# A decoder layer's output projection as seven products of quarters, with the gating branch's values and mixing moved behind the first stage

## The chip, the cores and the metric

The kernel runs on one core of a Trainium2 chip. A core has a tensor engine for matmuls (TensorE, PE in the profile; its loading of stationary operands is PEld), three engines for elementwise work, VectorE (DVE), ScalarE (ACT) and GpSimd (POOL), and a queue engine, SyncE (SP), from which nearly all loads are issued here. Each engine works through its own list of instructions in order; between engines, semaphores say when an operand is ready or a buffer free. The metric is the device time of one execution in microseconds. Less is better.

## The reference

One layer over 512 tokens of width 2048. All arithmetic is in float32.

```python
shift, scale, gate = split(silu(c) @ w_ada + b_ada, 3)
h = rms_norm(x, norm_g) * (1 + scale) + shift
u, v, g_a, q, k, v_b, g_b, f = split(h @ w_in)    # 7 parts of 1024 columns, 16 of f
# A: 8 channel groups of 128; v normalized over its 1024 channels, then mixed over
#    the 128 tokens of a chunk by a lower-triangular matrix per group
y_a = gelu(u) * (mix(layer_norm(gelu(v)), tril(w_s)) + b_s) * silu(g_a)
# B: 16 heads of 64, causal attention, logits biased by the running sum of log sigmoid(f + b_f)
y_b = forgetting_attention(q, k, v_b, f) * silu(g_b)
y = concat([y_a, y_b]) @ w_out                    # (512, 2048) @ (2048, 2048)
out = rms_norm(x + gate * y, final_g)
```

## The kernel before

Every float32 matrix product is done as three matmuls in a rounded format: each operand is split into a rounded part (hi) and the remainder (lo), and hi·hi, lo·hi and hi·lo are added up in PSUM. So each weight tile goes through three steps in `w_tile` (L117): a load from HBM to a `raw` buffer (a ring of 4), a copy to hi on ScalarE (L129), a subtraction for lo on VectorE (L130), or on GpSimd in the first stage. hi and lo have two buffers each. A weight tile of 128x1024 is 512 KB. The activations are split the same way (`split`, L65 to L67) and kept: `hh`/`hl` for the normalized input, `yh`/`yl` for the concatenated branches, 16 blocks of 128 channels x 512 tokens each.

Products come in two layouts. `col_group` (`mm_cols`, L145 to L147) puts 128 output columns on the partitions and the 512 tokens on the free axis; `mm_toks` (L154 to L156) puts 128 tokens on the partitions and up to 512 columns on the free axis. Either way a matmul is 128x128 by 128x512.

The program runs in these stages:

1. Normalization and transposition of x, and the sums for shift and scale.
2. The first stage (names `s`, 28 to 191 us): u and most of gate A, 14 blocks of columns, paced by loads. u becomes `y[0..7]`, gated in place.
3. `v_group(0)`, `qk_group(0)`, `g_group(0)`, then for u = 1, 2, 3 `g_group(u)`, `qk_group(u)`, `v_group(u)`: the B branch, four heads per u. After each `qk_group` the attention's steps go into a list `slots`; one entry is popped per weight tile (`tick`, L133), so attention runs among the products. Another list, `fillers`, is popped in the same way and holds `spatial_weights` (L607: loads, masks, transposes and splits the mixing matrices) at u = 1 and then the sums for the output gate (L593, L594, on GpSimd, 276 to 523 us). Attention's result is multiplied by gate B (`sgB`) and becomes `y[8..15]`.
4. The values of branch A (`va`, 610 to 706 us): 16 weight tiles, GELU, layer norm; the square root's reciprocal is a power on GpSimd (L91).
5. The last two blocks of gate A (`ga`, 706 to 730 us), with the normalization (`norm_half`), the mixing (`mix_head`, L731 to L743) and the splits of y (`split_y`) among them and at the start of stage 6.
6. The output projection (`wo`): for column groups g = 0, 1, 2 of 512 columns, eight weight tiles of two channel blocks by `mm_toks` into four banks (128 tokens each). `wo_evac` (L775) multiplies by the gate (L785), adds x (L791), squares and sums on ScalarE (L793) and multiplies by `final_g` (L795), all elementwise work in SBUF on VectorE.
7. Column group 3 is done token block by token block (L833 to L835) from weights `w3` that were loaded and split ahead, so that only the last block's scaling follows the last matmul: sum of squares, a power on GpSimd (L841), scaling (L842 to L847), output.

A scheduler sets the order on every engine. It walks the program with estimated times and priorities; weight tiles have a raised one (`WPRI`) and evacuations of PSUM too (`EPRI`), so they may be put ahead of work that was written earlier. The order lists below show what came out.

## Time and profile before

| | us |
|---|---|
| median of 3 runs | 920.67 (920.17 to 920.79) |
| the profiled execution | 922.11 |
| its span | 920.4 |
| TensorE busy in it | 898.9 |
| VectorE, ScalarE, GpSimd busy | 528.7, 412.4, 326.4 |
| mean granted TensorE clock | 0.988 of full |

The profile is of one execution, whose own time stands in the table beside the span from its first to its last recorded instruction. "L154 PE MATMUL wo<-whi_wo,yh" is line 154's matmul into the tile `wo`; after the shapes come the count, the busy sum and the mean of one in nanoseconds, then the idle time ahead and what ended it. In a timeline the first two numbers are the start and the length in microseconds; a bracket gives the idle time ahead and its releaser. In a window row the length comes first, then for PE, PEld, DVE, ACT and POOL the busy time and the count, then the clock, the share of the DMA engines and GB/s. A row of waits gives the sum, the count and the longest.

### The profile page before, as it was taken

The page shows a single profiled execution, that of the slowest core. Times are in us where ns is not written, and L with a number is a line of the kernel's source. Part 1 is how long each engine was busy: PE and PEld are TensorE (multiplying, and loading weights), DVE is VectorE, ACT ScalarE, POOL GpSimd, SP SyncE. Part 2 cuts the span into 40 slices and gives each one's busy share as a digit, 9 for nine tenths or more (in the row PEclk, how much of TensorE's full clock was granted, in tenths as well). Part 3 has the DMA queues.
Part 4 walks back from the last instruction along what each step waited for, and adds up shares of the span by engine and source line. Part 5 has one row for each costly group of instructions (what it writes and reads, how often), then busy time and mean ns, then how long its engine had stood idle before and what let it go on. Part 6 is the DMA issues. An engine that isn't in the chain of part 4 may idle for free.

```text
span 920.4 us, 12414 instructions
## 1 busy us (share of the span) xinstructions
PE 898.9 (98%) x4504; PEld 763.0 (83%) x4504; DVE 528.7 (57%) x886; ACT 412.4 (45%) x724; POOL 326.4 (35%) x238
## 2 busy tenths in 40 slices
...
PEclk8899999999999999999999999999999999999999
...
GB/s 341 352 353 355 354 302 189 76 89 136 94 114 115 130 170 145 154 150 127 160 172 179 144 81 107 78 70 92 71 107 97 81 125 105 149 180 196 69 104 92
DMA packets 113821, 142.74 MB, mean 155 GB/s; under 512 B 8400, under 2 KB 85408, under 8 KB 113248
## 3 DMA queue, kind: packets, MB, share of 16 engines
...
HBM read 137.54 MB, written 4.19 MB: 154 GB/s over the span
## 4 chain that ended last, share of the span: by engine, by line
PE 95%; DMA 2%; issue 1%; DVE 1%; ACT 0%; SPq 0%; POOLq 0%; POOL 0%; ACTq 0%; DVEq 0%
PE s L145 6%; PE s L147 6%; PE s L146 6%; PE wo L156 5%; PE wo L154 5%; PE wo L155 5%; PE vb L155 3%; PE vb L156 3%; PE vb L154 3%; PE k L145 3%; PE k L147 3%; PE gb L145 3%; PE gb L146 3%; PE k L146 3%; PE va L156 3%; PE gb L147 3%
## 5 line engine op out<-in xcount | busy, mean ns | idle before, releaser
L593 POOL TENSOR_SCALAR gate<-gate,sc 128x512 f32<-128x512 f32 x60 | 104.4, 1750 | 37.4 <-DMA gate<-in_w_ada_dram 34.5
L130 POOL TENSOR_TENSOR wlo_st<-raw_st,whi_st 128x1024 fp32r<-128x1024 f32 (+3 forms) x36 | 68.5, 1904 | 59.6 <-ACT whi_st L129 55.7
L145 PE MATMUL s<-hh,whi_st 128*128 128x512 f32 x224 | 88.0, 396 | 1.4 <-ACT hh L267 1.4
L146 PE MATMUL s<-hl,whi_st 128*128 128x512 f32 x224 | 88.1, 393 | 0.0
L594 POOL TENSOR_TENSOR gate<-gate,gate 128x512 f32<-128x512 f32 x60 | 86.5, 1442 | 2.1
L244 DVE SCALAR_TENSOR_TENSOR acc<-ada,sc,acc 128x512 f32<-128x512 f32 x98 | 73.9, 755 | 5.8 <-DMA ada<-in_w_ada_dram 3.1
L147 PE MATMUL s<-hh,wlo_st 128*128 128x512 f32 x224 | 76.4, 395 | 0.0
L154 PE MATMUL wo<-whi_wo,yh 128*128 128x512 f32 x192 | 74.8, 390 | 0.0
L155 PE MATMUL wo<-whi_wo,yl 128*128 128x512 f32 x192 | 74.7, 389 | 0.0
L155 PE MATMUL vb<-whi_vb,hl 128*128 128x256 f32 (+1 forms) x256 | 72.1, 287 | 0.0
L154 PE MATMUL vb<-whi_vb,hh 128*128 128x256 f32 (+1 forms) x256 | 71.8, 286 | 0.0
L156 PE MATMUL wo<-wlo_wo,yh 128*128 128x512 f32 x192 | 70.0, 390 | 0.0
L156 PE MATMUL vb<-wlo_vb,hh 128*128 128x256 f32 (+1 forms) x256 | 67.7, 285 | 0.0
L91 POOL TENSOR_TENSOR rsv<-rsv,nhalf 128x1 f32<-128x1 f32 x4 | 4.6, 1150 | 166.1 <-DVE rsv L90 166.1
L129 ACT ACTIVATE whi_st<-raw_st 128x1024 fp32r<-128x1024 f32 (+3 forms) x36 | 31.2, 870 | 66.3 <-PE s L146 40.9
L841 POOL TENSOR_TENSOR sfin<-sfin,nhalf 128x1 f32<-128x1 f32 x4 | 2.2, 549 | 149.0 <-DVE sfin L838 149.0
L145 PE MATMUL k<-hh,whi_k 128*128 128x512 f32 x128 | 51.1, 399 | 1.8 <-DVE q L445 1.8
L145 PEld LDWEIGHTS s<-hh,whi_st 128*128 128x128 f32 x224 | 42.6, 191 | 10.1 <-ACT hh L267 1.5
L146 PE MATMUL q<-hl,whi_q 128*128 128x512 f32 x128 | 50.7, 396 | 0.0
L145 PE MATMUL q<-hh,whi_q 128*128 128x512 f32 x128 | 50.4, 394 | 0.0
L146 PE MATMUL gb<-hl,whi_gb 128*128 128x512 f32 x128 | 50.3, 393 | 0.0
L145 PE MATMUL gb<-hh,whi_gb 128*128 128x512 f32 x128 | 50.3, 393 | 0.0
...
## 6 DMA issues: line engine op xcount, KB each, us to landing
ada<-in_w_ada_dram SPq DMA_DIRECT2D x128, 256.0 KB
...
```

Of the source, the lines that this page charges most:

```text
L91: nc.gpsimd.tensor_tensor(dst, dst, nhalf[:, 0:1], ALU.pow)
L129: nc.scalar.activation(hi, raw, AF.Copy)
L130: (loeng or nc.vector).tensor_tensor(lo, raw, hi.bitcast(F32), ALU.subtract)
L145: nc.tensor.matmul(pt, hi[:, j, cs], hh[k], start=(k == first), stop=False)
L146: nc.tensor.matmul(pt, hi[:, j, cs], hl[k], start=False, stop=False)
L147: nc.tensor.matmul(pt, lo[:, j, cs], hh[k], start=False, stop=(k == last))
L154: nc.tensor.matmul(o, ah[k][:, tsl], hi[:, j, :], start=(k == first), stop=False)
L155: nc.tensor.matmul(o, al[k][:, tsl], hi[:, j, :], start=False, stop=False)
L156: nc.tensor.matmul(o, ah[k][:, tsl], lo[:, j, :], start=False, stop=(k == last))
L244: nc.vector.scalar_tensor_tensor(sb if kk == KB - 1 else a, ga[:, j], col, a, ALU.mult, ALU.add)
L593: nc.gpsimd.tensor_scalar(ga[:, j], ga[:, j], sc[:, kk : kk + 1], None, ALU.mult)
L594: nc.gpsimd.tensor_tensor(a, a, ga[:, j], ALU.add)
```

## The change

The output projection is written as a product of 2x2 blocks and computed with seven block products instead of eight, by a known scheme. Rows of y are halved into tokens 0 to 255 and 256 to 511, channels into branch B's 1024 ("1") and branch A's ("2"), and for each pair of column groups (g1, g2) = (0, 1), (2, 3), called a unit, the weights into B11, B12 (branch B's rows), B21, B22 (branch A's). The left-hand blocks needed are A11, A12, A22 and four sums, S1 to S4; the right-hand ones B11, B21, B22 and four sums. The names p1 to p7 are those of the products: A11·p1, A12·p2, S4·p3, A22·p4, S1·p5, S2·p6, S3·p7. Each product is 256 tokens x 1024 channels x 512 columns in two banks (V, Z or X).

- **Left-hand sums.** `split_b` turns the second token half of `y[8+i]` into a difference on GpSimd before it is split; `sums` makes S1, S2, S4 from y in place on VectorE and splits them into buffers of q and k, which are free by then.
- **Right-hand sums.** p7 needs B12 and B22, loaded to `raw`, and B12 - B22 in a tile T (L912, VectorE), which is split; then T becomes B11 - T, is split again for p6 without a load, serves p5 (B22 loaded again, minus T), and becomes B21 - T for p4. Subtractions for p5 and p4 are half on VectorE, half on GpSimd. lo of p1, p2, p3, p6 is half on GpSimd as well. There are 24 loads of 512 KB per unit, 48 in all, where there were 32.
- **Alternation.** The first two products go step by step, a step of A11·p1 and one of S3·p7, since p7's T takes p1's B11 too; A12·p2 and A22·p4 likewise with B21.
- **Evacuation.** V and Z of the first two products are copied by ScalarE (c1, c7); sums u2, u3 and c7 are made on VectorE and GpSimd; gating, adding x (now on GpSimd) and squares follow per block of tokens. In unit 1 S4·p3 comes last, token block by token block, from `w3` split ahead.
- **Order of the stages.** The values (`va_products`) with `spatial_weights` come right after the first stage, and normalization and mixing lie in the slots of `v_group(0)`. The constant rows of q and k (`heads_tiles`, memsets on GpSimd) follow that. `g_group(3)` comes last before the projection, after `ga`; attention of u = 3 then ends before its gate is there, and `evac_gb` multiplies `y[14]`, `y[15]` later.

TensorE, start of the projection. Before (`wo0_t` is the bank of 128 tokens t, `whi_wo0_8` the first weight tile, `yh8` branch B's first block):

```order
L154 MATMUL wo0_0_6725<-whi_wo0_8_6731,yh8_6691 128x512
L155 MATMUL wo0_0_6725<-whi_wo0_8_6731,yl8_6692 128x512
L156 MATMUL wo0_0_6725<-wlo_wo0_8_6732,yh8_6691 128x512
L154 MATMUL wo0_0_6725<-whi_wo0_8_6731,yh9_6695 128x512
L155 MATMUL wo0_0_6725<-whi_wo0_8_6731,yl9_6696 128x512
L156 MATMUL wo0_0_6725<-wlo_wo0_8_6732,yh9_6695 128x512
```

The same place now, the second step of unit 0 (`woV` is A11·p1, `woZ` S3·p7):

```order
L849 MATMUL woV0_0_6811<-whi_p1_0_1_6884,yh10_6664 128x512
L850 MATMUL woV0_0_6811<-whi_p1_0_1_6884,yl10_6665 128x512
L849 MATMUL woV0_1_6812<-whi_p1_0_1_6884,yh10_6664 128x512
L850 MATMUL woV0_1_6812<-whi_p1_0_1_6884,yl10_6665 128x512
L849 MATMUL woZ0_0_6813<-whi_p7_0_1_6918,yh10_6664 128x512
L850 MATMUL woZ0_0_6813<-whi_p7_0_1_6918,yl10_6665 128x512
L849 MATMUL woZ0_1_6814<-whi_p7_0_1_6918,yh10_6664 128x512
L850 MATMUL woZ0_1_6814<-whi_p7_0_1_6918,yl10_6665 128x512
L851 MATMUL woV0_0_6811<-wlo_p1_0_1_6885,yh10_6664 128x512
L851 MATMUL woV0_1_6812<-wlo_p1_0_1_6885,yh10_6664 128x512
```

A step has 24 matmuls from two weight tiles of two blocks, as many as one weight tile had before; half of them wait for p7.

VectorE in the same steps, now (`ta0` is T, `p1_0_0` a raw tile of B11, `b12_0_1` and `b22_0_1` the raw tiles of the second step, `sgA`/`sgB` the gates):

```order
L67 TENSOR_TENSOR wlo_p7_0_0_6855<-ta0_6845,whi_p7_0_0_6854 128x512 x2
L355 SCALAR_TENSOR_TENSOR y6_1740<-sgA6_6611,y6_1740 128x512
L346 SCALAR_TENSOR_TENSOR sgA7_6616<-th_a7_6617,ga_1_6338 128x512
L346 SCALAR_TENSOR_TENSOR sgB6_6797<-th_b6_6798,gb3_0_6621 128x512
L912 TENSOR_TENSOR ta0_6845<-p1_0_0_6815,ta0_6845 128x512 x2
L355 SCALAR_TENSOR_TENSOR y7_1811<-sgA7_6616,y7_1811 128x512
L912 TENSOR_TENSOR ta0_6845<-b12_0_1_6912,b22_0_1_6914 128x512 x2
L441 TENSOR_TENSOR y14_6378<-y14_6378,sgB6_6797 128x512
L346 SCALAR_TENSOR_TENSOR sgB7_6802<-th_b7_6803,gb3_1_6622 128x512
L67 TENSOR_TENSOR wlo_p1_0_1_6885<-p1_0_1_6882,whi_p1_0_1_6884 128x512
L67 TENSOR_TENSOR wlo_p7_0_1_6919<-ta0_6845,whi_p7_0_1_6918 128x512 x2
```

Before, one L130 subtraction stood there per weight tile; now six operations per step make p7's operand and T, among the gatings of the last blocks of both branches.

VectorE at the end, before (`r3_3` is the last column group of the last 128 tokens):

```order
L785 TENSOR_TENSOR r3_3_7964<-wo3_3_7710,gate_141 128x512
L791 TENSOR_TENSOR r3_3_7964<-r3_3_7964,xr3_3_7966 128x512
L838 SCALAR_TENSOR_TENSOR sfin_6724<-ssf_6723,sfin_6724 128x1
L842 SCALAR_TENSOR_TENSOR r3_3_7964<-r3_3_7964,sfin_6724,fg3_7761 128x512
L845 TENSOR_SCALAR r0_3_7073<-r0_3_7073,sfin_6724 128x512
```

And now (`tmp0` and `tmp1` are the evacuations of the last product for token blocks 0 and 1, `c70`, `u30` blocks 2 and 3):

```order
L864 TENSOR_TENSOR tmp0_8236<-woZ1_0_7578,gate_141 128x512
L1020 TENSOR_SCALAR sfin_6808<-sfin_6808 128x1
L891 TENSOR_SCALAR c70_0_7084<-c70_0_7084,sfin_6808 128x512
L891 TENSOR_SCALAR u30_0_7184<-u30_0_7184,sfin_6808 128x512
L1035 TENSOR_TENSOR wide_7849<-tmp0_8236,wide_7849 128x512
L891 TENSOR_SCALAR c70_1_7085<-c70_1_7085,sfin_6808 128x512
L891 TENSOR_SCALAR u30_1_7185<-u30_1_7185,sfin_6808 128x512
L1037 SCALAR_TENSOR_TENSOR sfin_6808<-ssf_6807,sfin_6808 128x1
L889 SCALAR_TENSOR_TENSOR wide_7849<-wide_7849,sfin_6808,fgb_7282 128x512
L891 TENSOR_SCALAR c10_0_7080<-c10_0_7080,sfin_6808 128x512
L864 TENSOR_TENSOR tmp1_8280<-woZ1_1_7579,gate_141 128x512
```

The last evacuation now has the scaling of the other three token blocks ahead of it.

The diff, cut to its core:

```diff
...
+            if b > 5:
+                nc.vector.tensor_tensor(y[8 + b], y[8 + b], sg, ALU.mult)
...
+    fillers.append(spatial_weights)
+    va_products()
+    slots.extend([
+        [c_(norm_half, 0)],
+        [c_(mix_head, 0), c_(mix_head, 1)],
+        [c_(mix_head, 2), c_(mix_head, 3)],
+        [c_(norm_half, 1)],
+        [c_(mix_head, 4), c_(mix_head, 5)],
+        [c_(mix_head, 6), c_(mix_head, 7)],
+    ])
+    v_group(0)
+    heads_tiles()
+    qk_group(0)
+    g_group(0)
+    for u in range(1, 4):
...
+        if u < 3:
+            g_group(u)
+        qk_group(u)
+        v_group(u)
...
+    def split_b(i):
+        b = y[8 + i]
+        nc.gpsimd.tensor_tensor(b[:, hi_half], b[:, hi_half], b[:, lo_half], ALU.subtract)
+        split_y(8 + i)
 
     def split_y(k):
         yh[k] = act.tile([P, S], F32R, tag="hh", name=f"yh{k}")
         yl[k] = act.tile([P, S], F32R, tag="hl", name=f"yl{k}")
-        split(yh[k], yl[k], y[k], nc.gpsimd if k in (1, 3, 5, 7) else None)
-
-    norm_half(0)
-    c_ = lambda f, *a: (lambda: f(*a))
+        split(yh[k], yl[k], y[k], nc.gpsimd if k % 2 else None)
+    def sums(i):
+        b, a = y[8 + i], y[i]
+        nc.vector.tensor_tensor(b[:, hi_half], b[:, hi_half], a[:, hi_half], ALU.add)
+        nc.vector.tensor_tensor(b[:, lo_half], b[:, lo_half], b[:, hi_half], ALU.add)
+        sh_[i] = pb.tile([P, S], F32R, name=f"sh{i}", tag="qstk", bufs=8)
+        sl_[i] = pb.tile([P, S], F32R, name=f"sl{i}", tag="kstk", bufs=8)
+        split(sh_[i], sl_[i], b, nc.gpsimd if i % 2 else None)
+        nc.vector.tensor_tensor(b[:, lo_half], a[:, lo_half], b[:, hi_half], ALU.subtract)
+        s4[i] = act.tile([P, 2, H], F32R, name=f"s4_{i}", tag="ya", bufs=8)
+        split(s4[i][:, 0], s4[i][:, 1], b[:, lo_half])
...
+        [c_(split_b, i) for i in range(4)], [c_(split_b, 4), c_(split_b, 5)],
+        [c_(split_y, i) for i in range(4)], [c_(split_y, 4), c_(split_y, 5)],
     ])
-    col_group([(G0 + 768, 256)], [(lambda pt, b=b: evac_g(b, pt, pb)) for b in range(6, 8)], "ga")
-
-
-    KO = list(range(8, 16)) + list(range(8))
-    for k in KO[:8]:
-        split_y(k)
+    g_group(3)
+    slots.extend([
+        [c_(split_b, 6), c_(split_b, 7)], [c_(split_y, 6), c_(split_y, 7)],
+    ] + [[c_(sums, i)] for i in range(8)])
...
+    def wsplit(src, name, eng=None):
+        hi = wp.tile([P, 2, 512], F32R, tag="whi", name=f"whi_{name}")
+        lo = wp.tile([P, 2, 512], F32R, tag="wlo", name=f"wlo_{name}")
+        for j in range(2):
+            split(hi[:, j, :], lo[:, j, :], src[:, j, :], eng if j else None)
+        return hi, lo
...
+    def product(banks, kind, weights, begin, steps=range(4)):
+        for i2 in steps:
+            with tc.high_priority(offset=WPRI):
+                hi, lo = weights(i2)
+            for j in range(2):
+                for tt in range(2):
+                    i = 2 * i2 + j
+                    mm_part(banks[tt], kind, i, tt, hi[:, j, :], lo[:, j, :], begin and i == 0, i == 7)
             tick()
...
+        def minus(dst, a, b, pool=True):
+            for j in range(2):
+                (nc.gpsimd if j and pool else nc.vector).tensor_tensor(
+                    dst[:, j, :], a[:, j, :], b[:, j, :], ALU.subtract
+                )
+            return dst
...
+        def w_p1(i):
+            b11[i] = raw(1, g1, "p1", i)
+            return wsplit(b11[i], f"p1_{u}_{i}", nc.gpsimd)
+
+        def w_p7(i):
+            if i == 0:
+                t4 = pb.tile([P, 4, 512], F32, name=f"ta{u}", tag="vs")
+                T.extend([t4[:, 0:2, :], t4[:, 2:4, :]])
+                T.append(pb.tile([P, 2, 512], F32, name=f"tb{u}", tag="pth"))
+                T.append(pb.tile([P, 2, 512], F32, name=f"tc{u}", tag="ptl"))
+            minus(T[i], raw(1, g2, "b12", i), raw(0, g2, "b22", i), False)
+            w = wsplit(T[i], f"p7_{u}_{i}")
+            minus(T[i], b11[i], T[i], False)
+            return w
+
+        def w_p6(i):
+            return wsplit(T[i], f"p6_{u}_{i}", nc.gpsimd)
+
+        def w_p5(i):
+            a = raw(0, g2, "p5", i)
+            return wsplit(minus(a, a, T[i]), f"p5_{u}_{i}")
...
+        def w_p4(i):
+            return wsplit(minus(T[i], b21[i], T[i]), f"p4_{u}_{i}")
...
+        Z = [bank("mm" if u else "x", f"woZ{u}_{t}") for t in range(2)]
+        for i in range(4):
+            product(V, "A11", w_p1, i == 0, [i])
+            product(Z, "S3", w_p7, i == 0, [i])
+        c1 = tiles("c1", "yb", 8) if u else tiles("c1", "th")
+        evac(lambda t: nc.scalar.activation(c1[t], V[t], AF.Copy))
+        c7 = tiles("c7", "yb", 8) if u else tiles("c7", "p")
+        evac(lambda t: nc.scalar.activation(c7[t], Z[t], AF.Copy))
+        X = [bank("x", f"woX{u}_{t}") for t in range(2)]
+        product(X, "S2", w_p6, True)
...
+        evac(lambda t: nc.vector.tensor_tensor(u2[t], X[t], c1[t], ALU.add))
+        both(lambda t: nc.gpsimd.tensor_tensor(u3[t], u2[t], c7[t], ALU.add))
+        both(lambda t: nc.gpsimd.tensor_tensor(c7[t], c7[t], c1[t], ALU.add))
+        product(Z, "S1", w_p5, True)
+        evac(lambda t: nc.vector.tensor_tensor(u3[t], Z[t], u3[t], ALU.add))
...
+        for i in range(4):
+            product(V, "A12", w_p2, False, [i])
+            product(X, "A22", w_p4, False, [i])
+        evac(lambda t: gated(c1[t], V[t], g1))
+        evac(lambda t: nc.vector.tensor_tensor(c7[t], X[t], c7[t], ALU.add))
+        both(lambda t: gated(c7[t], c7[t], g1))
+        both(lambda t: piece(c1[t], t, g1))
+        both(lambda t: piece(c7[t], 2 + t, g1))
...
+        for t in range(2):
+            tk = 2 + t
+            s0, s1 = sfin[:, tk, 0:1], sfin[:, tk, 1:2]
+            nc.vector.reduce_sum(s0, ssf[:, tk, 0:4], AX.X)
+            nc.vector.tensor_scalar(s1, s0, 1.0 / D, EPS, ALU.mult, ALU.add)
+            scale_out(tk, None)
...
+            tmp = pb.tile([P, S], F32, name=f"tmp{t}", tag="sgB", bufs=3)
+            gated(tmp, Z[t], g2)
+            nc.vector.tensor_tensor(u2[t], tmp, u2[t], ALU.add)
+            squares(u2[t], t, g2, tmp)
+            nc.vector.scalar_tensor_tensor(s1, ssf[:, t, g2 : g2 + 1], 1.0 / D, s0, ALU.mult, ALU.add)
+            scale_out(t, g2)
...
```

299 lines of the change are left out of this document (174 added, 125 removed).

## The prediction

> **What bounds the kernel now.** I read the busy shares first, then the clock row, then what TensorE (PE) waited for.
>
> ```profile
> span 920.4 us, 12414 instructions
> PE 898.9 (98%) x4504; PEld 763.0 (83%) x4504; DVE 528.7 (57%) x886; ACT 412.4 (45%) x724; POOL 326.4 (35%) x238
> PEclk8899999999999999999999999999999999999999
> PE xTp L313 <- DVE x L306: 6.1, 2, 5.2
> PE k L145 <- DVE q L445: 1.8, 1, 1.8
> PE cb L191 <- POOL cmask L74: 1.5, 1, 1.5
> ```
>
> TensorE is busy for 98% at nearly full clock. Of its waits, those behind L306 and L74 lie in the prologue, which the change leaves alone; one of 1.8 us lies in the middle. So a matmul saved is time saved, until another engine becomes late. The price of a matmul is the distance between starts:
>
> ```profile
> 895.00 0.39 PE L833 MATMUL wo<-w3h,yh 128*128 128x512 f32 x1
> 895.68 0.39 PE L833 MATMUL wo<-w3h,yh 128*128 128x512 f32 x1
> L154 PE MATMUL wo<-whi_wo,yh 128*128 128x512 f32 x192 | 74.8, 390 | 0.0
> L833 PE MATMUL wo<-w3h,yh 128*128 128x512 f32 x64 | 24.9, 389 | 0.0
> ```
>
> Three matmuls take 0.68 us, 0.227 each (the 390 ns of the groups is one from start to end, overlapping the next). The projection has 3 x (192 + 64) = 768: 174 us. How much cover the other engines have there (columns: length, then busy time of PE, PEld, DVE, ACT, POOL, clock, DMA share, GB/s):
>
> ```profile
> 706.00:730.00 24.00, 24.00 (x119) 20.25 (x118) 20.76 (x42) 12.60 (x19) 4.57 (x4) 1.00 0.32 106
> 782.00:825.00 43.00, 43.00 (x192) 35.60 (x191) 17.50 (x19) 12.02 (x15) 0.00 (x0) 1.00 0.45 153
> ```
>
> In the projection VectorE (DVE) works 41% of the time, GpSimd (POOL) not at all. Ahead of it, where mixing now starts, VectorE has 87%.
>
> **The matmuls.** Seven products of quarters have 7 x 8 x 2 x 3 = 336 matmuls per unit, 672 in two units: 96 fewer, 96 x 0.227 = **-21.8 us**. One product is 48 matmuls, 10.9 us. All else below is what VectorE, GpSimd and the loads do to this gain.
>
> **Prices of the added work.**
>
> ```profile
> 867.93 0.68 DVE L791 TENSOR_TENSOR r<-r,xr 128x512 f32<-128x512 f32 x1
> 868.53 0.69 DVE L795 TENSOR_TENSOR r<-r,fg 128x512 f32<-128x512 f32 x1
> L281 POOL TENSOR_TENSOR hl<-xT,hh 128x512 fp32r<-128x512 f32 x15 | 19.1, 1294 | 20.7 <-ACT xT L278 20.7
> ```
>
> A 128x512 operation costs VectorE 0.60 from start to start (a 256-wide one 0.33, estimated as half of it and a little), GpSimd 1.29. How they fare together is seen once, where GpSimd splits four tiles beside VectorE's work:
>
> ```profile
> 734.37 2.16 DVE L130 TENSOR_TENSOR wlo_wo<-raw_wo,whi_wo 128x1024 fp32r<-128x1024 f32 x1
> 735.41 6.95 POOL L67 TENSOR_TENSOR vl<-va,vh 128x512 fp32r<-128x512 f32 x4
> 737.45 0.86 DVE L735 SCALAR_TENSOR_TENSOR mt<-mix,cols,bias 128x256 f32<-128x256 f32 x2
> 738.24 1.26 DVE L743 TENSOR_TENSOR y<-y,mt 128x512 f32<-128x512 f32 x1
> 739.42 1.78 DVE L355 SCALAR_TENSOR_TENSOR y<-sgA,y 128x512 f32<-128x512 f32 x1
> 747.34 1.21 DVE L130 TENSOR_TENSOR wlo_wo<-raw_wo,whi_wo 128x1024 fp32r<-128x1024 f32 x1
> ```
>
> GpSimd's four took 1.74 each. VectorE's split of two blocks took 2.16 instead of 1.21, the two products 1.26 and 1.78 instead of 0.68: 2.6 us lost beside four to five GpSimd operations, with VectorE also on PSUM operands (L735, not slowed). I take **0.7 us of VectorE lost per GpSimd operation**; bounds 0 (no collision) and 1.29 (full exclusion).
>
> The Trainium skill (page "SBUF — State Buffer", section "SBUF: two separate sides") says that a VectorE operation with two SBUF inputs and a GpSimd operation that reads SBUF exclude each other for whole instructions. The rows above agree in direction, and their losses fit waits for whole instructions as well as sharing; if nothing overlaps, the result is the slower rival below.
>
> **Unit 0, first two products and S2·p6.** The order list has, from y6's gating to the last p6 split, 41 VectorE operations of 512 and 8 of 256: 41 x 0.60 + 8 x 0.33 = 27.2 us, and 16 operations on GpSimd. TensorE has 3 x 10.9 = 32.7. Bare, VectorE fits; with 16 x 0.7 = 11.2 it needs 38.4, 5.7 too much. Entry adds about 1.5, because the first split of p7 stands behind attention's last evacuation (o15) on VectorE. **+7**, from 3.5 (bare: the entry and two load delays of about 1) to 10.5 (0.9 per operation). S1·p5 and the A12·p2/A22·p4 pair have 34 operations, 20.4 us, and with some 14 GpSimd operations 30.2 against 32.7: hidden.
>
> **S4·p3 of unit 0.** VectorE 14 operations, 8.4, plus 8 x 0.7 = 14.0 against 10.9: 3.1 short, but much may be done early: **+1** (0 to 3).
>
> **Unit 1, first two products.** The ring of four raw tiles serializes the loads: B12 of a step waits for the first subtraction of the step before.
>
> ```profile
> 844.67 0.37 SPq L802 DMA_DIRECT2D raw_w<-in_w_out_dram  x1
> 848.42 1.06 ACT L66 ACTIVATE w3h<-raw_w 128x1024 fp32r<-128x1024 f32 x1 [4.08 <-DMA raw_w<-in_w_out_dram]
> ```
>
> From issue to use is 3.75. A step then costs 1.2 (subtraction of 2 x 0.60) + 0.4 (issue, as in the row) + 3.75, plus some 1.0 because the second load shares the engines: 6.3 against TensorE's 24 x 0.227 = 5.4. Four steps lose 3.4, entry 0.6. VectorE (25.2 us and 14 GpSimd operations x 0.7 = 35.0 against 32.7) runs beside it: **+4** (3 to 6). In all 48 loads of 512 KB run where there were 32: at the 45% of the window above, 16 more in less time would make some 75%, so bytes do not bind, latency does.
>
> **The tail.**
>
> ```profile
> 910.84 0.69 DVE L785 TENSOR_TENSOR r<-wo,gate 128x512 f32<-128x512 f32 x1 [6.64 <-PE wo L835]
> 911.57 0.69 DVE L791 TENSOR_TENSOR r<-r,xr 128x512 f32<-128x512 f32 x1
> 914.21 0.75 DVE L842 SCALAR_TENSOR_TENSOR r<-r,sfin,fg 128x512 f32<-128x512 f32 x1 [0.66 <-POOL sfin L841]
> 914.88 0.48 DVE L845 TENSOR_SCALAR r<-r,sfin 128x512 f32<-128x512 f32 x1
> ```
>
> Before, the last evacuation starts when TensorE ends, and 9.6 us follow. After, the last one (tmp1) stands on VectorE behind the scaling of blocks 2, 3 and 0. Counted from the end of X: blocks 2 and 3 are gated on VectorE by 3.1, GpSimd then adds block 3's residual (four in a row, done near 6.6) and u2's (8.3), then its powers; five VectorE operations follow until block 0's sum at 10.9; from there 1.95 (911.57+0.69 to 914.21), 0.67 and 0.48 to tmp1 at 14.0, while TensorE ends its 48 matmuls at 10.9. **+3.5** (0 if the residuals come early, to 4.5).
>
> **Values and mixing behind the first stage.**
>
> ```profile
> 191.00:216.00 25.00, 25.00 (x197) 24.84 (x196) 13.54 (x22) 8.27 (x15) 9.80 (x20) 1.00 0.48 129
> 715.12 2.66 POOL L91 TENSOR_TENSOR rsv<-rsv,nhalf 128x1 f32<-128x1 f32 x1 [4.10 <-DVE rsv L90]
> L419 POOL MEMSET q<- 128x512 f32 x4 | 2.1, 526 | 15.0 <-issue 15.0
> L614 POOL TENSOR_SCALAR_AFFINE_SELECT ws<-ws 128x1024 f32<-128x1024 f32 x1 | 1.9, 1864 | 57.7 <-DMA ws<-in_w_s_dram 57.7
> ```
>
> The first stretch of v_group(0) has VectorE free for 11 of 25 us; mixing brings about 14 more (16 + 16 mix operations at 0.40, four gatings, four splits), so it is nearly full. The split of weight tile vb0_2 now stands behind four normalizations that wait for GpSimd's powers (2.66 for one): late by 4.6 where TensorE has 3.0 of cover. **+1.5** (0 to 4). What moves along is covered: the selection of L614 and its one load run during the values, with GpSimd empty; the 16 memsets (8.3 us) go behind the four vl splits, since q's tiles are the values' buffers, and are due only at q's evacuation; the queue of SP issues 14 more loads in all, 0.37 each (issue row above). Gating, ga and gb(3) have VectorE near 30 of TensorE's 27; most of that runs early, and what doesn't is in unit 0's entry.
>
> **The wait that may go.**
>
> ```profile
> 345.54 0.47 PE L145 MATMUL k<-hh,whi_k 128*128 128x512 f32 x1 [1.84 <-DVE q L445]
> 349.46 0.42 PE L146 MATMUL k<-hl,whi_k 128*128 128x512 f32 x1
> 345.00:350.00 5.00, 4.46 (x13) 3.54 (x14) 3.92 (x5) 3.38 (x7) 4.21 (x4) 0.66 0.35 94
> ```
>
> Between these rows lie ten intervals in 3.92 us where 2.27 were due: after 1.84 idle the clock fell (0.66) and cost 1.65 more. Spatial weights leave this place: up to 3.4 gained, but VectorE's gb gating comes between instead: **-1.5** (-3.4 to 0). Each new wait that is as long costs the same 1.65; I expect one on average: **+1.7** (0 to 5, three).
>
> The Trainium skill (page "TensorE: Matmul & The Clock Gate", section "Part 1: The HAM clock gate") gives half clock only after an idle window of about 3.4 us; by it no wait here would cost clock and the sum would be 1.7 less. The 1.84 us row measures otherwise, and decides.
>
> **Sum.** -21.8 + 7 + 1 + 4 + 3.5 + 1.5 - 1.5 + 1.7 = -4.6. The span becomes 915.8; the profiled execution took 922.1, 1.4 above the median of 920.67, and lies 1.7 outside its span, so would be 917.5. Against the median: **916.1**. All bounds low give 902.0 (-18.7), all high 931.9 (+11.2).
>
> **Rivals.** *TensorE stays dense* (collisions small, as GpSimd's work falls where VectorE idles): stalls of 6 (unit 1's ring 3, tail 3) give 904.9. For it: 27.2 is under 32.7. Against: the rows at 734 to 741.
>
> *Exclusion on VectorE makes it slower.* Place: the splits of p7, p6 and p3, which TensorE waits for. At a loss x per GpSimd operation the stalls are 28.7 + 16x - 32.7 (unit 0 with its entry), 25.2 + 14x - 32.7 (unit 1) and 8.4 + 8x - 10.9 (p3). They sum to 38x - 14.0; with tail and clock (5.2), x = 0.8 makes 21.6, the whole gain, and decides; x = 1.05 gives 12.8 + 7.2 + 5.9 + 5.2 = 31.1, so **930**; full exclusion, 1.29, also delays the middle products and gives some 942. For it: 1.78 for 0.68 at 739.42 lost 1.1. Against: the mean over the stretch is 0.7.
>
> *No change*: stalls of 20 to 23.6, between these.
>
> *The change doesn't do what it says*: the moved pieces are plain in the order list; only the alternation could be undone by a late p7, which is in unit 0's term.
>
> **Chances.** Forecast (908 to 918.8) 0.34; dense (below 908) 0.18; no change, within 0.2% or 1.84 us (about what this kernel's measurement can tell), 0.16; exclusion 0.26 and other slower cases (entry, clock and tail all at their high ends) 0.06. Faster 0.52, same 0.16, slower 0.32. The likeliest one's own range is 908 to 919; 8 in 10 reach from 903 (under 5% below) to 931 (half of exclusion's upper part, 14%, above).
>
> **What would show it.** Of the profile after: TensorE's matmuls 4350 in number at 0.227; waits on p7's splits (L67, ta) and on L912 in unit 0, 5 to 9 us in all; on p7's loads in unit 1, 3 to 6; GpSimd splits of 1.6 to 1.8 us beside VectorE ones of over 0.68; tmp1 idle 3 us behind TensorE's end; one short wait at vb0_2; the 1.84 at k0 gone or smaller. Wrong I'd be if projection waits are under 6 or over 20, or if a stall of more than 4 stands in a place not named here.

## The result, and the profile after

The changed kernel takes **968.97 us** (median of 4 runs, 966.73 to 976.85) beside 920.73 for the one before in the same session: a ratio of **1.052 (1.044 to 1.060)**, slower by 48 us where 4.6 us of gain were forecast. Some executions of every kernel, the one before too, start with a lower clock and take 2 to 9 us longer for it; so traces are compared below by the projection's own length, not by the span, and the ratios of e15_seven_late and e16_plain_first, in whose session more than half of before's executions were of that kind, are flattering.

The page of the changed kernel, its totals and two rows of its slices:

```profile
span 967.0 us, 12710 instructions
...
PE 896.9 (93%) x4408; PEld 749.3 (77%) x4408; DVE 653.0 (68%) x1014; ACT 453.2 (47%) x827; POOL 473.5 (49%) x326
...
PE   6999999999999999999999999999996878887884
...
PEclk8899999999999999999999999999997889999998
```

TensorE has 96 matmuls fewer, as forecast, but its dense row breaks in the last quarter, which is the projection; VectorE has 128 instructions more than before, GpSimd 88. What TensorE waited for (sum, count, longest):

```profile
PE woV L851 <- DVE wlo_p L67: 11.7, 9, 4.0
PE woZ L851 <- DVE wlo_p L67: 10.5, 8, 2.9
PE woZ L849 <- ACT whi_p L66: 9.3, 4, 6.0
PE woX L851 <- DVE wlo_p L67: 8.9, 5, 3.2
...
PE q L145 <- DVE mt L739: 2.0, 1, 2.0
```

Four rows of the projection make 40.4 us, and 31.1 of it is the subtraction for the lo parts on VectorE. ScalarE's hi parts, the third row, wait in turn for T, which VectorE makes too. For GpSimd's lo parts TensorE waited only 1.8 us, so that these come late themselves is not what costs. The stretch from the last matmul of `g_group(3)` to the end, cut by product (length; PE, PEld, DVE, ACT, POOL busy; clock; DMA share; GB/s):

```profile
738.40:744.60 6.20, 0.19 (x2) 0.02 (x1) 3.79 (x7) 2.72 (x6) 4.19 (x3) 0.76 0.00 1
744.60:796.80 52.20, 41.87 (x144) 31.85 (x145) 45.39 (x56) 21.16 (x39) 26.94 (x16) 0.83 0.41 136
796.80:810.50 13.70, 11.80 (x49) 8.78 (x48) 12.83 (x11) 4.70 (x9) 10.26 (x7) 1.00 0.37 118
810.50:836.00 25.50, 22.62 (x97) 17.78 (x96) 20.47 (x23) 10.84 (x22) 14.54 (x10) 1.00 0.37 123
836.00:852.40 16.40, 13.11 (x49) 10.01 (x49) 15.61 (x15) 6.90 (x17) 12.65 (x8) 0.90 0.58 192
852.40:898.50 46.10, 35.46 (x145) 26.09 (x144) 36.46 (x41) 16.99 (x33) 20.55 (x13) 1.00 0.45 148
898.50:914.50 16.00, 13.02 (x50) 9.81 (x50) 13.97 (x13) 4.75 (x9) 10.20 (x7) 0.89 0.34 105
914.50:943.80 29.30, 23.67 (x97) 17.44 (x96) 26.73 (x26) 13.21 (x26) 20.54 (x13) 1.00 0.31 105
943.80:967.00 23.20, 11.08 (x49) 8.82 (x47) 16.19 (x30) 9.48 (x20) 10.68 (x10) 0.85 0.59 215
```

The rows are: the entry; unit 0's first two products with S2·p6; S1·p5; A12·p2 with A22·p4; S4·p3; then unit 1's first two products with S2·p6; S1·p5; A12·p2 with A22·p4; S4·p3 and the end. 48 matmuls are 10.9 us, 144 are 32.7. VectorE is busy for 79 to 95% of every row from 796.8 to 943.8, so no product has much cover. Against their matmuls the rows lose 6.2 and 19.5, 2.8, 3.7, 5.5, 13.4, 5.1, 7.5: 63.7 us.

### The profile page after: what moved, and what is told of

Read it like the earlier page. It is cut to its first block, busy times and chain, and to the rows that moved or that the text cites. A ratio compares the mean times of both kernels' runs of the same rounds, so it can differ in the third digit from the quotient of the medians.

```text
span 967.0 us, 12710 instructions
## 1 busy us (share of the span) xinstructions
PE 896.9 (93%) x4408; PEld 749.3 (77%) x4408; DVE 653.0 (68%) x1014; ACT 453.2 (47%) x827; POOL 473.5 (49%) x326
## 4 chain that ended last, share of the span: by engine, by line
PE 78%; DVE 11%; issue 3%; DMA 3%; POOL 2%; ACT 1%; SPq 0%; POOLq 0%; ACTq 0%; DVEq 0%
PE s L145 5%; PE s L147 5%; PE s L146 5%; DVE wlo_p L67 3%; PE vb L155 3%; PE vb L156 3%; PE vb L154 3%; PE q L145 3%; PE q L146 3%; PE q L147 3%; PE k L146 3%; PE va L156 3%; PE k L145 3%; PE k L147 3%; PE va L154 3%
## 5 line engine op out<-in xcount | busy, mean ns | idle before, releaser
L604 POOL TENSOR_SCALAR gate<-gate,sc 128x512 f32<-128x512 f32 x60 | 102.4, 1716 | 29.1 <-DMA gate<-in_w_ada_dram 23.8
L130 POOL TENSOR_TENSOR wlo_st<-raw_st,whi_st 128x1024 fp32r<-128x1024 f32 (+3 forms) x36 | 68.4, 1904 | 54.0 <-ACT whi_st L129 51.6
L605 POOL TENSOR_TENSOR gate<-gate,gate 128x512 f32<-128x512 f32 x60 | 93.0, 1552 | 1.9
L145 PE MATMUL s<-hh,whi_st 128*128 128x512 f32 x224 | 88.0, 396 | 1.4 <-ACT hh L267 1.4
L156 PE MATMUL vb<-wlo_vb,hh 128*128 128x256 f32 (+1 forms) x256 | 71.0, 286 | 0.0
L67 POOL TENSOR_TENSOR wlo_p<-p,whi_p 128x512 fp32r<-128x512 f32 x20 | 37.8, 1892 | 35.8 <-ACT whi_p L66 31.4
L145 PE MATMUL q<-hh,whi_q 128*128 128x512 f32 x128 | 50.5, 395 | 2.0 <-DVE mt L739 2.0
L66 ACT ACTIVATE whi_p<-p 128x512 fp32r<-128x512 f32 x56 | 32.3, 624 | 41.9 <-PE woZ L850 17.5
L145 PE MATMUL gb<-hh,whi_gb 128*128 128x512 f32 x128 | 50.9, 397 | 0.0
L145 PE MATMUL k<-hh,whi_k 128*128 128x512 f32 x128 | 50.7, 396 | 0.0
L67 DVE TENSOR_TENSOR ptl<-p,pth 128x512 fp32r<-128x512 f32 (+1 forms) x64 | 41.5, 672 | 13.5 <-ACT pth L66 12.3
L145 PEld LDWEIGHTS s<-hh,whi_st 128*128 128x128 f32 x224 | 42.6, 191 | 10.2 <-ACT hh L267 1.5
L154 PE MATMUL va<-whi_va,hh 128*128 128x512 f32 x128 | 50.3, 393 | 0.0
```

The lines of the kernel that those rows point to most:

```text
L66: nc.scalar.activation(hi, src, AF.Copy)
L67: (eng or nc.vector).tensor_tensor(lo, src, hi.bitcast(F32), ALU.subtract)
L130: (loeng or nc.vector).tensor_tensor(lo, raw, hi.bitcast(F32), ALU.subtract)
L145: nc.tensor.matmul(pt, hi[:, j, cs], hh[k], start=(k == first), stop=False)
L154: nc.tensor.matmul(o, ah[k][:, tsl], hi[:, j, :], start=(k == first), stop=False)
L156: nc.tensor.matmul(o, ah[k][:, tsl], lo[:, j, :], start=False, stop=(k == last))
```

## The experiments

"Length" is the time from the projection's first matmul to the end of its last, "after" what follows to the end of the span, both from the profiled execution. "Ratio" is to the kernel before in the same session. Medians are of 2 (e3_sequence) to 12 executions, of one in e4_probe. 672 matmuls at 0.227 would be 152.5; before, e1_front and e4_probe have 768 (174.3), e12_half to e14_late_both 720 (163.4).

| kernel | median us | ratio to before (95%) | length | after |
|---|---|---|---|---|
| before | 920.67 | | 179.0 | 9.6 |
| the change | 968.97 | 1.052 (1.044 to 1.060) | 210.3 | 12.1 |
| e1_front | 921.09 | 1.000 (0.996 to 1.003) | 174.8 | 9.0 |
| e2_all_vector | 934.38 | 1.016 (1.009 to 1.022) | 176.9 | 14.2 |
| e8_dose | 944.68 | 1.027 (1.017 to 1.037) | 191.2 | 12.2 |
| e4_probe | 919.03 | | 179.0 | 9.1 |
| e3_sequence | 983.16 | 1.066 (1.058 to 1.075) | 221.5 | 10.5 |
| e10_pool_direct | 962.98 | 1.043 (1.035 to 1.050) | 204.6 | 12.0 |
| e6_direct | 927.82 | 1.009 (1.004 to 1.013) | 170.3 | 13.9 |
| e5_whole | 942.41 | 1.020 (1.012 to 1.027) | 188.9 | 12.7 |
| e7_tail | 928.78 | 1.008 (1.004 to 1.011) | 175.8 | 13.1 |
| e9_best | 929.17 | 1.009 (1.005 to 1.013) | 173.2 | 14.1 |
| e11_no_sums | 917.21 | 0.994 (0.989 to 0.999) | 164.9 | 13.9 |
| e12_half | 929.42 | 1.009 (1.005 to 1.012) | 172.8 | 13.9 |
| e13_late_sums | 922.48 | 1.003 (0.999 to 1.006) | 170.9 | 13.9 |
| e14_late_both | 919.59 | 0.998 (0.994 to 1.001) | 170.8 | 11.4 |
| e15_seven_late | 925.83 | 1.001 (0.998 to 1.004) | 175.5 | 11.6 |
| e16_plain_first | 927.60 | 1.003 (1.000 to 1.007) | | |

The theory after the result: GpSimd's added operations and VectorE's take turns, so that VectorE's total time exceeds TensorE's shortened time. The rivals: the moved stages, the alternation of products, the ring of raw tiles, the tail.

**The moved stages alone.** The output projection of before, in 768 matmuls, behind the new order of stages:

```diff
-    for u in range(2):
-        unit(u)
+    KO = [8, 9, 10, 11, 12, 13] + list(range(8)) + [14, 15]
...
```

> The moved stages alone (values and mixing behind the first stage, the last gate group last), with the projection of before: 16 k blocks x 4 column groups, nothing left out. If the loss lies all in the projection, this is 920.7 within 4 us (by the changed kernel's trace the input products and mixing end some 3 us later than in the kernel before). If the moved stages carry part of it, 925 or more.

921.09: no change. The loss lies in the projection.

**GpSimd's elementwise work on VectorE.** All splits, subtractions, sums and additions that the change put on GpSimd, 92 instructions, 79 of them in the projection:

```diff
...
-            split(hi[:, j, :], lo[:, j, :], src[:, j, :], eng if j else None)
+            split(hi[:, j, :], lo[:, j, :], src[:, j, :])
...
-                (nc.gpsimd if j and pool else nc.vector).tensor_tensor(
+                nc.vector.tensor_tensor(
...
```

> The changed kernel with every elementwise operation that the projection had on GpSimd (79 of 128x512 or half of it) given to VectorE instead. Theory 'shared port' (a GpSimd operation and a VectorE operation with two SBUF inputs exclude each other): VectorE then needs 118 us (its own 209 operations at their bare prices) + 79 x 0.60 = 165 us instead of 199, its operations are back at 0.60 to 0.69 each, and the kernel takes 915 to 930. Theory 'too many operations on VectorE': 47 us more work for the late engine, so 990 or more. Theory 'loads come late': no change, 960 to 975.

934.38: giving VectorE *more* instructions made the kernel 34.6 us faster. That is 4 above the range of the theory 'shared port', and far from the other two. The same group of subtractions, in the change and then with all on VectorE (count, busy sum, mean ns, idle ahead), the latter with its page's totals:

```profile
L67 DVE TENSOR_TENSOR wlo_p<-p,whi_p 128x512 fp32r<-128x512 f32 x36 | 43.8, 1233 | 7.7 <-ACT whi_p L66 5.7 <-PE woX L851 2.0
...
L67 POOL TENSOR_TENSOR wlo_p<-p,whi_p 128x512 fp32r<-128x512 f32 x20 | 37.8, 1892 | 35.8 <-ACT whi_p L66 31.4 <-DVE tb L912 4.4
...
L996 DVE TENSOR_TENSOR c<-woX,c 128x512 f32<-128x512 f32 x4 | 2.7, 685 | 0.6 <-PE woX L851 0.5
```

```profile
PE 888.2 (95%) x4408; PEld 747.7 (80%) x4408; DVE 634.1 (68%) x1106; ACT 452.6 (49%) x827; POOL 320.8 (34%) x234
...
L67 DVE TENSOR_TENSOR wlo_p<-p,whi_p 128x512 fp32r<-128x512 f32 x54 | 35.3, 684 | 2.5 <-ACT whi_p L66 2.5
```

36 instructions took 43.8 us where 54 take 35.3. With 92 instructions more, VectorE is busy for 18.9 us less (634.1 after 653.0); in the projection itself it is busy for 161.4 us, where the theory had 165. VectorE operations with one operand in PSUM (L996, 685 ns) were not slowed. A timeline of the change shows how it comes about:

```profile
777.52 0.68 DVE L912 TENSOR_TENSOR p<-p,ta 128x512 f32<-128x512 f32 x1
777.65 1.70 POOL L912 TENSOR_TENSOR p<-p,ta 128x512 f32<-128x512 f32 x1 [1.21 <-DVE wlo_p L67]
778.12 1.77 DVE L912 TENSOR_TENSOR tc<-p,tc 128x512 f32<-128x512 f32 x1
779.31 1.73 POOL L912 TENSOR_TENSOR p<-p,tb 128x512 f32<-128x512 f32 x1
779.82 1.77 DVE L67 TENSOR_TENSOR wlo_p<-tc,whi_p 128x512 fp32r<-128x512 f32 x1
781.00 1.74 POOL L67 TENSOR_TENSOR wlo_p<-ta,whi_p 128x512 fp32r<-128x512 f32 x1
781.51 1.78 DVE L912 TENSOR_TENSOR p<-p,ta 128x512 f32<-128x512 f32 x1
...
784.61 0.68 DVE L912 TENSOR_TENSOR tc<-p,tc 128x512 f32<-128x512 f32 x1
```

While GpSimd has work in its queue, each engine completes one operation per 1.7 us. So the pair does in 1.7 us two operations for which VectorE alone takes 2 x 0.60 = 1.2.

**The price by itself.** The kernel before, with idle work on GpSimd beside the projection's splits: two-input additions in column group 1, one-input multiplications in group 2.

```diff
+                    if g == 1:
+                        nc.gpsimd.tensor_tensor(jp, last_raw[0][:, 0, :], last_raw[0][:, 1, :], ALU.add)
+                    else:
+                        nc.gpsimd.tensor_scalar(jp, last_raw[0][:, j, :], 2.0, None, ALU.mult)
```

> The kernel before with idle GpSimd work added to its projection: for the first four weight tiles of column group 1, two additions of 128x512 with two SBUF inputs, of column group 2, two multiplications by a constant (one SBUF input); nobody waits for them. Shared port: VectorE's lo splits of 128x1024 (two SBUF inputs, 1.22 us alone) grow to 2 to 3.5 us beside the additions; beside the multiplications they stay at 1.22 if one input doesn't take the port, or grow as well if it does. No port: all stay at 1.22. The time stays at 921 within 2 us either way.

919.03 in one run: there is room for idle work there. The trace gives the price:

```profile
779.44 1.22 DVE L131 TENSOR_TENSOR wlo_wo<-raw_wo,whi_wo 128x1024 fp32r<-128x1024 f32 x1
...
783.64 1.29 POOL L822 TENSOR_TENSOR jp<-raw_wo 128x512 f32<-128x512 f32 x1 [23.15 <-DVE r L798]
784.10 1.91 DVE L131 TENSOR_TENSOR wlo_wo<-raw_wo,whi_wo 128x1024 fp32r<-128x1024 f32 x1 [0.68 <-ACT whi_wo L130]
785.01 2.14 POOL L822 TENSOR_TENSOR jp<-raw_wo 128x512 f32<-128x512 f32 x1
...
794.92 1.29 POOL L822 TENSOR_TENSOR jp<-raw_wo 128x512 f32<-128x512 f32 x1
794.98 2.31 DVE L131 TENSOR_TENSOR wlo_wo<-raw_wo,whi_wo 128x1024 fp32r<-128x1024 f32 x1 [4.01 <-ACT whi_wo L130]
...
816.68 1.49 POOL L824 TENSOR_SCALAR jp<-raw_wo 128x512 f32<-128x512 f32 x1 [2.44 <-DMA raw_wo<-in_w_out_dram]
816.74 1.63 DVE L131 TENSOR_TENSOR wlo_wo<-raw_wo,whi_wo 128x1024 fp32r<-128x1024 f32 x1 [1.35 <-ACT whi_wo L130]
```

A split of 1.22 takes 1.91 and 2.31 when it meets an addition (0.7 and 1.1 lost), where 2 to 3.5 were expected. Who waits for whom can be read off the ends. The first split ends 1.08 us behind the end of the addition that started before it (784.93 and 786.01), the second likewise (796.21 and 797.29); the addition at 785.01, which started during a split, ends 1.14 behind that split (786.01 and 787.15). The two additions that started first took 1.29, as alone. So these are waits for a whole instruction, which the rows of the prediction could not tell from sharing. Beside a multiplication with one input the split takes 1.63 (0.4 lost) and ends only 0.2 behind it (818.17 and 818.37): an operation with one input on GpSimd collides too, but here the split didn't wait for all of it.

**The dose.** How the loss grows with the number of operations on GpSimd. As e2_all_vector, but 24 sums and residual additions stay on GpSimd:

```diff
...
-        nc.vector.tensor_tensor(rr, rr, xr, ALU.add)
+        (eng or nc.gpsimd).tensor_tensor(rr, rr, xr, ALU.add)
...
```

> Between the changed kernel (79 of the projection's operations on GpSimd, 969.0) and the one with none (934.4): the 24 output sums and residual additions stay on GpSimd, the weights' work and the splits of y go to VectorE. If each operation on GpSimd costs VectorE about the same (34.6 us / 79 = 0.44 net each), 934.4 + 24 x 0.44 = 945, within 940 to 949. If only the splits that TensorE waits for matter, 932 to 937 (the output sums are waited for by nobody soon).

944.68, 10.3 more for 24 operations: 0.43 us of the kernel's time each; the change's 79 cost 34.6, 0.44 each. At these two doses the loss goes with the number of GpSimd operations, the output's sums as much as the weights' splits.

**Alternation.** The products one after the other, B11 and B21 loaded again:

```diff
...
-        for i in range(4):
-            product(V, "A11", w_p1, i == 0, [i])
-            product(Z, "S3", w_p7, i == 0, [i])
+        product(V, "A11", w_p1, True)
+        product(Z, "S3", w_p7, True)
...
```

> The changed kernel with its products one after the other instead of alternating; B11 and B21 are loaded a second time for it (16 loads of 512 KB more). If the alternation, with its chain p1 -> T -> p7 in a ring of four raw tiles, holds the first pairs up (they lost 6 + 19.5 and 13.4 us), this is 945 to 960. If the port is the cause, VectorE has the same operations: 962 to 975.

983.16, 14 slower than the change and above both ranges. Undoing the alternation at the price of 16 more loads doesn't help, so nothing speaks for it as the cause; what it costs by itself isn't separated from the loads.

**The ring of raw tiles.** B12 loaded straight into T, so that two of a step's three loads pass through the ring; once with all on VectorE, once as the change has it:

```diff
-            minus(T[i], raw(1, g2, "b12", i), raw(0, g2, "b22", i), False)
+            if u or i:
+                wget(T[i], 1, g2, i)
+                minus(T[i], T[i], raw(0, g2, "b22", i), False)
+            else:
+                minus(T[i], raw(1, g2, "b12", i), raw(0, g2, "b22", i), False)
```

> All elementwise work of the projection on VectorE, and B12 loaded straight into the tile T (from the second step on), so that a step takes two raw tiles of the ring of four instead of three and its loads don't wait for the subtraction of the step before. If the load ring holds the first pair of products up (my term of 4 us in unit 1, some of it in unit 0), 927 to 932. If VectorE alone does, 933 to 936.

> The changed kernel with its work on GpSimd as it is (969.0), and only B12 loaded straight into T. With the port contended VectorE takes 199 us for the projection and is late everywhere, so a better load ring gives at most what it gave without contention (6.6 us): 962 to 970. If loads and contention multiply each other, under 960.

6.6 and 6.0 us better (6.6 and 5.7 by the projection's length): the loss by the ring is there, of about the same size in both, so loads and collisions don't multiply each other.

**Longer instructions.** e2_all_vector with one 128x1024 operation where two of 128x512 stood, on VectorE for the lo parts and T and on ScalarE for the hi parts:

> All elementwise work of the projection on VectorE, and the weights' splits and subtractions as one instruction of 128x1024 (1.14 us from start to start) instead of two of 128x512 (1.20). With 56 + 32 such pairs per unit less 8, VectorE has some 5 us less to do. If VectorE's throughput is what still holds the projection up (934.4 measured), this is 927 to 933. If the first half's earlier readiness mattered more than the throughput, 934 to 942.

942.41, 8 worse, in line with the second theory: what TensorE waits for is the first half, and it comes later. That isn't shown by itself, and with B12 straight into T the longer instructions cost nothing (e7_tail beside e9_best, next).

**The end.** e6_direct with a raised priority for the last evacuations, with the longer instructions (e7_tail) and without (e9_best):

```diff
-            gated(tmp, Z[t], g2)
-            nc.vector.tensor_tensor(u2[t], tmp, u2[t], ALU.add)
+            with tc.high_priority(offset=EPRI):
+                gated(tmp, Z[t], g2)
+                nc.vector.tensor_tensor(u2[t], tmp, u2[t], ALU.add)
...
```

> Both of these together (whole-tile instructions, B12 straight into T), and the last two evacuations with a raised priority, so that tmp1 stands ahead of the scaling of other token blocks. The tail term was 3.5 us (tmp1 begins 3.1 us behind TensorE's end in the changed kernel). If the three are what is left beside the port, they add up to 10 to 15 us: 920 to 926, the kernel before within its interval. If something else holds (VectorE still has some 160 us to do beside 152 us of TensorE, with the start of the projection crowded), 926 to 932.

> All elementwise work of the projection on VectorE, B12 loaded straight into T, and the last evacuations with a raised priority (without the whole-tile instructions, which cost 8 us). TensorE's last matmul ends at 910.6 in the version without the priority, as in the kernel before (910.8), but 13.9 us follow it there and 9.6 in the kernel before. If the tail term is what tmp1's place costs, 3 to 4 us go: 922 to 925. If the outputs' transfers hold the end, no change: 926 to 929. Faster than the kernel before (under 918.5) would mean that VectorE is no longer what sets the pace.

928.78 and 929.17, no gain over e6_direct. There the last evacuation already begins at 910.67, as the last matmul ends (910.63), so the priority had nothing to move. What is longer than before is the way from VectorE's last operation to the end of the span: 7.9 us (916.63 to 924.5) instead of 5.0 (915.36 to 920.4), as the outputs are still being written (383 GB/s from 916.6 to 922.5).

**Without the left-hand sums.** The kernel leaves out S1, S2 and S4, so its output is another.

```diff
-    ] + [[c_(sums, i)] for i in range(8)])
+    ])
...
```

> All elementwise work of the projection on VectorE, B12 straight into T, and S1, S2, S4 left out: the products S1.p5, S2.p6 and S4.p3 take parts of y as they are, so the output is another, but TensorE has the same matmuls. VectorE has 8 x (3 x 0.33 + 0.60 + 0.33) = 15 us less to do, all around the projection's start. If VectorE's work at the start is what is left (927.8 without this), 914 to 922. If it is elsewhere (unit 1, tail), 925 to 928.

917.21: 10.6 of e6_direct's time goes with making S1, S2 and S4, on VectorE and with hi copies on ScalarE, whether by the amount of this work or by its place.

**Half the scheme.** Columns 0 to 1023 by plain products, the seven products for the rest, all elementwise work of their unit on VectorE (four splits of y stay on GpSimd, as in the kernel before):

```diff
+    for g in range(2):
+        wob = [bank("x" if g == 1 else "mm", f"wo{g}_{t}") for t in range(NT)]
...
-    for u in range(2):
-        unit(u)
+    unit(1)
```

> Half of the output columns (0 to 1023) by plain products first, then one unit of seven products, all elementwise work of it on VectorE, B12 straight into T. The plain half needs only 16 splits of 1.14 us in 87 us, so the left-hand sums (15 us, worth 10.6 us at the start of the other version) are done beside it. 48 matmuls fewer: -10.9 us. Against it: unit 1 lost 3.4 us to TensorE's waits in the version with two units (831 to 910.6 where 76.2 were due), and the end 4.3 us (13.9 behind the last matmul instead of 9.6). Sum -3.2: 917.5, and 914 to 920. If VectorE is too late even so, 921 to 926.

929.42: nothing gained over e6_direct, and above both ranges. Its entry shows one reason (VectorE ahead of the projection's first matmul, and that matmul):

```profile
745.87 0.41 DVE L787 TENSOR_TENSOR y<-y,y 128x256 f32<-128x256 f32 x1
746.20 0.75 DVE L67 TENSOR_TENSOR sl<-y,sh 128x256 fp32r<-128x256 f32 x2
746.87 0.41 DVE L797 TENSOR_TENSOR y<-y 128x256 f32<-128x256 f32 x1
...
748.50 0.69 DVE L346 SCALAR_TENSOR_TENSOR sgA<-th_a,ga 128x512 f32<-128x512 f32 x1
...
749.24 0.80 PE L154 MATMUL wo<-whi_wo,yh 128*128 128x512 f32 x1 [4.36 <-DVE sgA L346]
```

Sums (L787, L67 `sl`, L797) that no product needs for 16 weight tiles (16 x 24 x 0.227 = 87 us) stand on VectorE ahead of `sgA`, which TensorE waits for. Next, each sum behind the subtraction of the weight tile written before it (e13), and in the last unit token blocks 2 and 3 finished and sent out first (e14):

```diff
+        with tc.issue_after(newest_lo[0].ins):
+            nc.vector.tensor_tensor(a[:, hi_half], a[:, hi_half], b[:, hi_half], ALU.add)
```

> As e12_half, but each sum of the left-hand blocks stands on VectorE behind the lo subtraction of the weight tile that was written before it, so behind the gatings of the last blocks of both branches, and no longer ahead of them. Nothing else differs: the same number of operations and matmuls. Theory 'place' (the sums cost because they stand ahead of an operand that TensorE waits for at the projection's entry): the stall of 4.4 us behind sgA goes and with it the half clock after it (ten or so matmuls at 0.43 instead of 0.227, some 2 us), so 929.4 - 6.4 = 923 (921 to 926). Theory 'amount' (VectorE has too much to do in the projection, wherever it stands): the time only moves to a later wait, and it stays at 927 to 931.

> As e13_late_sums, and in the last unit the 128-token blocks 2 and 3 are evacuated, finished and sent out before blocks 0 and 1 of the same column group are evacuated, with raised priority, so that their output transfers start while the last product still runs. Theory 'the end is set by output transfers that start late': TensorE's last matmul is followed by some 10 us, as before the change, instead of 14.3: 4 less than e13_late_sums, 919 if the sums' place is the cause. Theory 'the end is set by the work of the last block itself': no more than 1 less than e13_late_sums.

922.48, as 'place' said: the entry's wait is gone. 919.59, 2.9 less where 'late transfers' had 4 and its rival at most 1: 11.4 us follow the last matmul instead of 13.9, and from VectorE's last operation (911.01) to the end of the span (915.9) it is 4.9 again. The projection's waits of e14_late_both sum to 4. It is level with the kernel before (0.994 to 1.001), not shown faster.

**The whole scheme, well placed.** The same for all seven products in both units, with A12·p2 right after the first two products of unit 0:

```diff
+        if u == 0:
+            product(V, "A12", w_p2, False)
         X = [bank("x", f"woX{u}_{t}") for t in range(2)]
         product(X, "S2", w_p6, True)
```

> All four column groups in seven products again (672 matmuls, as the change), all elementwise work of the projection on VectorE, B12 loaded straight into T, and now: the left-hand sums S1, S2, S4 stand on VectorE behind the weights' subtractions that were written before them and start three weight tiles later; in the first unit A12*p2 runs right after the first two products, so that S2*p6, the first product that needs a sum, comes 10.9 us later (B21 is loaded a second time for p4, 4 loads more); in the last unit the token blocks 2 and 3 are finished and sent out before blocks 0 and 1. Theory 'place' (VectorE's 186 us fit beside TensorE's 152 only in the mean; what cost was operations ahead of a waited-for operand): e6_direct's 927.8 loses most of the 10.6 that leaving the sums out gained, and the 4 of the end: 914 (911 to 918). Theory 'amount': with 48 more matmuls saved than in the half version but twice the sums and right-hand pieces, VectorE stays behind TensorE: 921 to 926.

925.83, some 0.5% above the 920.67 of before. The entry is clear (the first matmul at 736.46, with no wait), but the time came back behind it. A stretch of unit 0, from the second step of the first two products through A12·p2 and S2·p6 to S1·p5, then the whole length of the projection; last, for comparison, that of e14_late_both:

```profile
745.00:801.00 56.00, 51.60 (x209) 38.87 (x207) 56.00 (x109) 30.85 (x58) 0.00 (x0) 0.97 0.41 135
736.46:911.97 175.51, 164.15 (x673) 125.61 (x671) 169.33 (x303) 87.74 (x170) 2.10 (x2) 0.98 0.50 167
...
733.67:904.47 170.80, 166.68 (x721) 134.08 (x719) 135.65 (x241) 75.83 (x143) 3.46 (x3) 1.00 0.41 136
```

VectorE is busy for 56.0 of 56.0 us, and in the whole projection for 169.3 us beside 152.5 of matmuls. (The 186 in the expectation is the change's figure, with its collisions; without them it was too much as well, 160.8 in e6_direct.) In the half version it is busy for 135.7 beside 163.4. So 'amount' holds for the whole scheme, as far as these orders go, and 'place' for the half. A variant that starts unit 0 with A11·p1 alone:

> As e15_seven_late, but the first unit begins with A11*p1 alone, then the first step of S3*p7, A12*p2, and the rest of S3*p7 (B11 is loaded a second time, 4 loads more): at the entry VectorE has 2 subtractions per weight tile instead of 6 per two, while the last gatings run. If the stalls that remain at the entry come from p7's pieces crowding the last gatings there, 2 to 4 less than e15_seven_late; if the entry is clear already, the same within 1.5, or up to 2 more from the extra loads.

927.60: no better than e15_seven_late. No trace of it is used here.

## Why the prediction was wrong

**What held.** The matmuls: -21.8 at 0.227 each. (The 4350 among the signs was a slip: 4504 less 96 is 4408, which came.) Each load's latency in the ring: +4 for one unit, 6.0 to 6.6 for both. The tail's mechanism, to a fraction of a microsecond:

```profile
954.49 0.39 PE L851 MATMUL woZ<-w3l,s 128*128 128x512 f32 x1
...
958.01 0.68 DVE L864 TENSOR_TENSOR tmp<-woZ,gate 128x512 f32<-128x512 f32 x1
```

tmp1 starts 14.2 us behind X's end (943.8) where 14.0 were forecast; the end came 2.5 later than before's instead of 3.5.

**What came out by luck.** The moved stages with the q wait: forecast 0 net, measured 0 (e1_front), but not by the steps named. In v_group(0), where 1.5 were put at vb0_2, no wait of TensorE is over 0.5 us. The k wait of 1.84 is gone, and one of 2.0 stands at q instead, behind the mixing (`PE q L145 <- DVE mt L739`). The mixing's load on VectorE was added up wrongly as well (32 x 0.40 and eight of 0.60 make 17.6, not 14), but no term hangs on it.

**The failed step: "hidden", with a VectorE that never waits.** The forecast set VectorE's work beside TensorE's and let a loss arise only where the first was longer in a product or two: 5.7 us in unit 0's first products, 3.1 in its S4·p3, 2.3 in unit 1's first products. S1·p5 and the pair were "hidden", so put at nothing. For the products that its terms cover, all but the last one (13 x 48 matmuls, 141.6 us), VectorE was to need 38.4 + 30.2 + 14.0 + 35.0 and, for unit 1's middle, which has no term, 30.2 again: 147.8 us. So added up it was 6 us over already. The trace of the same products, and the largest of VectorE's waits there behind each kind of releaser (sum, count, longest):

```profile
744.60:943.80 199.20, 161.54 (x624) 121.76 (x625) 171.45 (x182) 78.56 (x148) 115.69 (x71) 0.94 0.40 134
...
DVE wlo_p L67 <- ACT whi_p L66: 8.1, 7, 3.1
DVE p L912 <- DMA p<-in_w_out_dram: 3.4, 2, 2.0
...
DVE wlo_p L67 <- PE woX L851: 2.7, 2, 2.0
```

VectorE was busy for 171.5 us, 23.7 more than that, and it idled for 27.8 us, nearly all of it in waits: 11.7 behind loads, 8.8 behind ScalarE's hi parts, 6.6 behind TensorE's products. With the 6 us these make the 57.6 by which the stretch is longer than its matmuls; the forecast had 12. In the products called hidden VectorE was busy for 33.3 us (796.8 to 836.0), and for 40.7 in the same products of unit 1 (898.5 to 943.8, where the splits of `w3` are made too), instead of 30.2 beside 32.7. When VectorE has no reserve, the time in which it waits itself is lost to TensorE as well, and this the forecast put at next to nothing. The sum is read from one trace; that each microsecond of idling cost one isn't shown by a run of its own.

| term | forecast | measured |
|---|---|---|
| unit 0, first products and S2·p6, with the entry | +7 | 6.2 + 52.2 - 32.7 = +25.7 |
| S1·p5 and the pair, unit 0 | 0, "hidden" | +6.5 |
| S4·p3 of unit 0 | +1 | +5.5 |
| unit 1, first products and S2·p6 | +4 | +13.4 |
| S1·p5 and the pair, unit 1 | no term | +12.6 |
| tail | +3.5 | +2.5 |
| front and q wait | 0 | +1.9 in this execution: 738.4 against 730.0 + the 6.5 of gate columns and mixing that lay behind it before |

With -21.8 the right column makes +46.3; the spans differ by 46.6. Half clock, 1.7 in the forecast, is contained in the rows: 48 times the next matmul started more than 0.38 us after the last without a wait between, which makes some 10 us. The prediction's own sign of being wrong, waits of over 20 in the projection, came with 40.

**The mis-sized term: 0.7 us per GpSimd operation.** Of the 23.7 us that VectorE was busy beyond the forecast, most is this price. Between 744.6 and 943.8 VectorE did 172 operations of 512 and 9 of 256, 106.2 us at the forecast's bare prices, where its terms have 101.6. It took 171.5 beside 71 GpSimd operations, where the terms have 66. So each of these cost 0.92: 4.6 us come from VectorE's count, 3.5 from GpSimd's, 15.6 from the price. In runs like that from 777.52 it is 1.1. That is inside the stated bounds; the 0.7 was a mean over a stretch in which VectorE partly read PSUM, which isn't slowed. The rival "exclusion on VectorE" had the mechanism, and the right row (739.42). But its price of 1.05 gave no more than 930, as it too held VectorE free of waits and the middle products covered.

The Trainium skill (page "SBUF — State Buffer", section "SBUF: two separate sides") describes an exclusive lock between a VectorE operation with two SBUF inputs and a GpSimd operation that reads SBUF. The traces agree for GpSimd's operations with two inputs: 1.77 and 1.74 in turns in the change, one waiting for the other's end in e4_probe, PSUM operands unharmed; beside those with one input (0.4 lost) the wait was not for the whole instruction. What the sum lacked was the other side of it, that offloading to GpSimd then makes next to nothing parallel: 34.6 us were gained by taking it back.

**The rest.** Of the 48 us, 34.6 go when GpSimd's share is taken back (e2_all_vector; the collisions cost more, since VectorE then has 79 operations to do in their place) and 6.6 with the ring (e6_direct). That leaves 927.8, which is 28.9 above 898.9, the time before less 21.8. The left-hand sums are 10.6 of it (e11_no_sums), the end about 4.3 (13.9 after the last matmul instead of 9.6). The remaining 14 were not taken apart; VectorE's other work, late first operands and half clock are in it.
